# Scores' PSUM as one tile of two banks with a single buffer, in a two-layer hybrid attention backbone

## The chip, the cores and the metric

The kernel runs on one core of one Trainium2 chip. The metric is the device time of one execution in microseconds (us), as a median of several runs. PE is the matmul engine (TensorE; PEld is its weight loads, which overlap it), DVE the vector engine, ACT the scalar engine, POOL is GpSimd, and SP issues the DMAs. Scores are accumulated in PSUM, which here holds eight banks of 2 KB in each partition.

## The reference

Two layers (`DEPTH = 2`) work on 256 latent tokens and 256 context tokens of width 1024. Each projects its modulated input once and gives the columns to three groups of heads. Their outputs are concatenated, projected by `w_out` and followed by a convolutional FFN. The last layer computes latent tokens alone.

```python
def _diff_attend(q, k, v, lam, scale):                       # A: 6 heads, two maps per head, 32 wide
    s = jnp.einsum('bhqcd,bhkcd->bhcqk', q, k) * scale
    p = jax.nn.softmax(s, axis=-1)
    p = p[:, :, 0] - lam * p[:, :, 1]
    return jnp.einsum('bhqk,bhkd->bhqd', p, v)

# B: 6 heads, 64 wide, neighbourhood window with a bias, and all context keys, in one softmax
s = jnp.concatenate([s_win + bias (masked), s_ctx], axis=-1)
p = jax.nn.softmax(s, axis=-1)

# C: 4 heads, 96 wide, from low-rank q and kv
s = jnp.einsum('bhqd,bhkd->bhqk', q, k) * scale
p = jax.nn.softmax(s, axis=-1)
```

## The kernel before

**Stages.** Each layer first computes the modulation and the input projections, then attends in the order C, A, B, and then multiplies with `w_out` and runs the FFN. Every large product in split precision is three matmuls (`mm3`, lines 134 to 136): high by high, low by high, high by low. Group A has three pairs of heads `i`, whose two maps per head count as the two banks of a group. Group B has three pairs, whose two heads are the banks. Group C has two pairs.

**A scores group.** For one block of 128 queries `score3` issues six matmuls, three for each bank. The two banks' matmuls use different rows of the matmul array (32 or 64 of 128). Then comes, for each bank, a softmax (`softmax_rows`): DVE takes the negated maximum (L381), ACT the exponential with its row sum (L384), DVE the reciprocal (L385) and the scaling (L674; in A L701 to L703 instead, which put the two maps together). In B, latent queries first get the bias added in PSUM (L745). PE then transposes the probabilities (L392), ACT copies them out of PSUM (L393), and PE multiplies them with v (L400). A group is 512 keys wide for latent queries and 256 for context queries, which only layer 0 has.

**PSUM.** The eight banks are shared among four tags: `acc` three, `ada` one, `sc` two, `tp` two. Each call of `scp()` takes the next of the two `sc` banks, and waits until whoever used it last has read it:

```python
    def bank(tag, bufs):
        return ps.tile([P, 512], F32, tag=tag, name=tag, bufs=bufs)
...
    def scp():
        return bank("sc", 2)
```

The two banks also serve `proj_vk` (four token blocks), the early projections behind the FFN and the context modulation `evb`.

**Order.** A scheduler decides where each instruction stands on its engine. It knows the tiles and their buffers and fills the time between the dependent steps of attention with matmuls that wait for nothing: projections of the next pairs in A (the 256- or 512-column `acc` products), and the `w_out` products (`acc<-whi,mixhi` and their kin) in B. An engine runs its instructions strictly in that order.

Of the kernel before, what the change touches and what calls it, by code (L numbers as in the profile page):

```python
# [8 lines left out]
F32 = mybir.dt.float32  # L9
# [20 lines left out]
CTX, LAT = slice(0, 256), slice(256, 512)  # L30
# [47 lines left out]
def build(nc, tc, st, I, out):  # L78
    P = 128
# [9 lines left out]
    ps = st.enter_context(tc.tile_pool(name="ps", bufs=1, space=PSUM))  # L89
    dp = st.enter_context(tc.tile_pool(name="dp", bufs=1, space=bass.MemoryType.DRAM))  # L90

    V, S, G, T = nc.vector, nc.scalar, nc.gpsimd, nc.tensor

    def bank(tag, bufs):
        return ps.tile([P, 512], F32, tag=tag, name=tag, bufs=bufs)

    def acc():
        return bank("acc", 3)
# [2 lines left out]
        return bank("ada", 1)  # L101

    def scp():
        return bank("sc", 2)

    def tpp():
        return bank("tp", 2)

    def load(dst, src):
        nc.sync.dma_start(out=dst, in_=src)  # L110
# [14 lines left out]
    def split_from(src, hi, lo):  # L125
        S.copy(hi, src)
        V.tensor_tensor(lo, src, hi.bitcast(F32), ALU.subtract)
# [5 lines left out]
    def mm3(o, lh, ll, rh, rl, first, last):  # L133
        T.matmul(o, lhsT=lh, rhs=rh, start=first, stop=False)  # L134
        T.matmul(o, lhsT=lh, rhs=rl, start=False, stop=False)  # L135
        return T.matmul(o, lhsT=ll, rhs=rh, start=False, stop=last).ins  # L136
# [21 lines left out]
    LO, HI = list(range(4)), list(range(4, KD))  # L158
    early = {}
# [107 lines left out]
    def pump(n):  # L267
        while n and pend:
            try:
                next(pend[0])  # L270
                n -= 1
            except StopIteration:
                pend.pop(0)
# [105 lines left out]
    def softmax_rows(sc, nk, ap, tag):  # L379
        nm = sm.tile([P, 1], F32, tag="nm", name="nm")  # L380
        V.reduce_max(nm, sc[:, 0:nk], axis=AX.X, negate=True)  # L381
        p = ap.tile([P, 512], F32, tag=tag, name="p", bufs=2)
        sums = sm.tile([P, 2], F32, tag="sums", name="sums")
        hT["exp"] = S.activation(p[:, 0:nk], sc[:, 0:nk], AF.Exp, bias=nm, accum_out=sums[:, 0:1]).ins  # L384
        V.reciprocal(sums[:, 1:2], sums[:, 0:1])  # L385
        return p, sums
# [53 lines left out]
    def split_early(raw):  # L440
        hi = lp.tile([P, 1280], F32R, tag="ehi", name="ehi", bufs=2)
        lo = lp.tile([P, 1280], F32R, tag="elo", name="elo", bufs=2)
        split_from(raw, hi, lo)
        return kview((hi, lo), 2)
# [45 lines left out]
    nxt = load_round(1)  # L490
    ada_round(0, raws)
    ef = [acc() for _ in EF]
    evb = {pr: scp() for pr in (1, 0)}
    for s in range(4):
        ks = (2 * s, 2 * s + 1)
        w = split_early(wes[s])
# [39 lines left out]
    for l in range(L):  # L536
        last = l == L - 1
# [15 lines left out]
        pr = sm.tile([P, 2, 32], F32, tag="lampr", name="lampr", bufs=2)  # L553
# [43 lines left out]

        def proj_vk():
            w = vkw
            for t in (2, 3, 0, 1):  # L600
                tok = slice(128 * t, 128 * t + 128)
                po = acc() if last and t % 2 else scp()
                for k in range(KD):
                    hi, lo = w[k // 3 * 3]
                    mm3(po[:, 0:288], hT["hi"][:, k, tok], hT["lo"][:, k, tok], hi[:, k % 3, :], lo[:, k % 3, :],
                        k == 0, k == KD - 1)
                pump(PF)
                S.copy(vt[:, t, 256:544], po[:, 0:288])
# [13 lines left out]
        def score3(banks, q, k, rows, r0, qs, nk):  # L622
            for t, (a, b) in enumerate(((0, 0), (0, 1), (1, 0))):
                for n, sc in enumerate(banks):
                    r = slice(r0 + rows * n, r0 + rows * n + rows)
                    T.matmul(sc[:, 0:nk], lhsT=q[r, a, qs], rhs=k[r, b, 0:nk], start=t == 0, stop=t == 2,  # L626
                             tile_position=(r.start, 0))
# [39 lines left out]
        def simple_fin(k):  # L667
            def f(po, c):
                split_from(po, mix[0][:, k, c], mix[1][:, k, c])
            return f  # L670

        def normed(sc, nk):
            p, s = softmax_rows(sc, nk, ap, "p0")
            V.tensor_scalar_mul(p[:, 0:nk], p[:, 0:nk], s[:, 1:2])  # L674
            return p
# [19 lines left out]

        def attn_a(i):
            def sco(h, e, qs, qt, nk, name):
                banks = [scp() for _ in range(2)]
                score3(banks, aqs[i], aks[i], 32, 64 * e, qs, nk)
                (p0, s0), (p1, s1) = [softmax_rows(sc, nk, ap, f"p{m}") for m, sc in enumerate(banks)]  # L700
                V.tensor_tensor(s1[:, 1:2], s1[:, 1:2], lam[:, 2:3], ALU.mult)  # L701
                V.tensor_scalar_mul(p1[:, 0:nk], p1[:, 0:nk], s1[:, 1:2])
                V.scalar_tensor_tensor(p0[:, 0:nk], p0[:, 0:nk], s0[:, 1:2], p1[:, 0:nk], ALU.mult, ALU.add)  # L703
                return p0

            def fin(po, c):
                sq = ap.tile([P, 256], F32, tag="sq", name="sq", bufs=2)
                S.activation(sq, po, AF.Square)
                pm = tpp()
                T.matmul(pm[:, 0:256], lhsT=K["bones"], rhs=sq, start=True, stop=True)  # L710
                S.activation(sq, pm[:, 0:256], AF.Ln, bias=epsc)
                S.activation(sq, sq, AF.Exp, scale=-0.5)
                V.scalar_tensor_tensor(sq, po, nw[:, 0:1], sq, ALU.mult, ALU.mult)
                split_from(sq, mix[0][:, i, c], mix[1][:, i, c])

            heads(i, sco, vt, 0, fin)
# [13 lines left out]
        def attn_b(i):  # L730
            banks = []

            def sco(h, e, qs, qt, nk, name):
                if e == 0:
                    banks[:] = [scp() for _ in range(2)]
                    score3(banks, bqs[i], bks[i], 64, 0, qs, nk)
                sc = banks[e]
                if name == "lat":
                    bt = ap.tile([P, 256], F32, tag="rpb", name="rpb", bufs=3)
                    load(bt, I["rpb"][l, h, qt])  # L740
                    b3 = bt.rearrange("p (a c) -> p a c", c=64)
                    with tc.issue_after(hT["pow"]):
                        G.tensor_tensor(b3, b3, K["m01"].unsqueeze(1).to_broadcast([P, 4, 64]), ALU.mult)
                    G.tensor_tensor(b3, b3, K["mneg"].unsqueeze(1).to_broadcast([P, 4, 64]), ALU.add)
                    V.tensor_tensor(sc[:, LAT], sc[:, LAT], bt, ALU.add)  # L745
                return normed(sc, nk)

            heads(i, sco, vt, 416 if i else 384, simple_fin(3 + i))
# [23 lines left out]
        mq, mk = [], []  # L772
# [53 lines left out]
                S.copy(mq[h // 2][64:96, h % 2, :], q[32 * h:32 * h + 32, qc])  # L826

        def attn_c(i):
            def sco(h, e, qs, qt, nk, name):
                sc = scp()  # L830
                T.matmul(sc[:, 0:nk], lhsT=mq[i][0:96, e, qs], rhs=mk[i][0:96, e, 0:nk], start=True, stop=True)  # L831
                return normed(sc, nk)

            heads(i, sco, vm, 0, simple_fin(6 + i))

# [93 lines left out]
        def post(pl, b, t):  # L929
            r = rsum[t]  # L930
            y, rs = pst.pop(t)
            hT["dv"] = V.scalar_tensor_tensor(xr[t], y, rs[:, 0:1], b, ALU.mult, ALU.add, accum_out=r[:, 2:3]).ins
            pst[t] = centred(xr[t], (r[:, 2:3], r[:, 3:4]), pl, jt(pl))
# [210 lines left out]
        if not last:  # L1144
            free = [h1.tile([P, KD, 512], F32R, tag=n, name="ada" + n).bitcast(F32).rearrange("p k c -> p (k c)")
                    for n in ("hi", "lo")]
            sc = Slices(free[0], [free[1][:, 1024 * i:1024 * i + 1024] for i in range(4)])
# [9 lines left out]
        def tail2(ts):  # L1157
            if last:
                return
            for t in ts:  # L1160
                post(pq, b2, t)
            hold = ExitStack()
            if 2 in ts:
                flush()
                new_h()
            else:
                for i in (12, 13, 14):
                    w = kview(wsplit(I["w_f"][l + 1, i], 1024), KD)
                    early[i] = (acc() if i < 14 else scp(), w, [(CTX, LO + HI)] if i == 14 else [])
                    f_mm(early[i][0], w, 0, LO + HI, LAT, True, i < 14)  # L1170
                w = {kb: kview(wsplit(I["w_v"][l + 1, 0, kb], 1024), 4) for kb in range(2)}
                early["v"] = ({1: scp(), 0: acc()}, w, LO + HI, (0,))
                for e in range(2):
                    r = v_mm(early["v"][0][1], w, LO + HI, 1, e, True, True)
                hold.enter_context(tc.issue_after(r))
            with hold:
                for t in ts:
                    modulated(pq, l + 1, False, t, xr[t], sums=pst.pop(t))
# [101 lines left out]
```

## Time and profile before

| | |
|---|---|
| median of 3 runs | 1155.72 us (1154.95 to 1156.66) |
| profiled execution | 1158.58 us, of which 1156.5 us are the span of its trace |
| PE busy | 1107.0 us, 96% of the span |
| DVE, ACT busy | 836.1 us (72%), 591.2 us (51%) |
| mean granted PE clock | 0.986 of full speed |

PE is busy nearly all the time, so what counts is which of its time is useful, and where the other engines would hold it up. Busy time of PE includes the modelled end of each matmul; from start to start the same matmuls take a little less. In layer 0 attention lies between 118 and 316.5 us (C to 159.3, A to 261.7, B to 316.5), in layer 1 A and B lie between 824.9 and 943.2 us.

### The profile page before, as it was taken

What the parts mean: (1) busy time and instruction counts of PE and PEld (TensorE: products, weight loads), DVE (VectorE), ACT (ScalarE), POOL (GpSimd) and SP (SyncE); (2) the same over time, 40 slices, a digit from 0 to 9 for tenths busy, and PEclk for the clock granted to TensorE, in tenths of its full rate; (3) what the DMA queues carried; (4) which work ended last, traced back from release to release, by engine and by line L of the source; (5) the groups of instructions that cost most, each with busy time, mean ns of one, the idle gap of its engine ahead of it and who ended that gap; (6) DMA issues with size and microseconds to landing.
All of it is one profiled execution on the core that took longest, in us unless ns stands there. A gap on an engine that the chain in (4) does not pass through costs nothing.

```text
span 1156.5 us, 17907 instructions
## 1 busy us (share of the span) xinstructions
PE 1107.0 (96%) x6776; PEld 902.1 (78%) x6776; DVE 836.1 (72%) x1505; ACT 591.2 (51%) x1063; POOL 83.8 (7%) x104
## 2 busy tenths in 40 slices
PE   5999999999998999999999999999999979999997
PEld 3877666686778888887888877897778758999985
DVE  4544677757588887986977687666766777888755
ACT  4345556656548644444352245555555656666541
POOL 0000100003123000000000002110000420000000
PEclk9999999999999999999999999998999988999999
DMA  9767112112143554643558894533111333555662
GB/s 362 295 241 279 58 37 74 37 37 86 51 164 97 197 169 144 199 152 116 186 174 309 311 328 131 176 94 99 53 55 56 128 132 121 183 183 188 201 203 89
DMA packets 58213, 179.19 MB, mean 155 GB/s; under 512 B 7024, under 2 KB 12432, under 8 KB 58128
## 3 DMA queue, kind: packets, MB, share of 16 engines
q1 hardware_dynamic: 58128, 178.05, 45.8%
q8 instruction: 54, 0.88, 0.3%
q14 instruction: 31, 0.25, 0.1%
HBM read 176.94 MB, written 1.08 MB: 154 GB/s over the span
## 4 chain that ended last, share of the span: by engine, by line
PE 85%; DVE 6%; ACT 2%; issue 2%; POOL 2%; DMA 2%; SPq 0%; DVEq 0%; POOLq 0%; ACTq 0%
PE acc L134 21%; PE acc L135 21%; PE acc L136 21%; PE sc L626 6%; PE tp L392 3%; PE tp L400 3%; PE sc L831 2%; DVE wlo L122 1%; PE sc L134 1%; PE sc L135 1%; PE sc L136 1%; POOL xn L344 1%; DMA rawr<-in_w_ada_e 1%; PE ada L234 1%; PE ada L136 1%
## 5 line engine op out<-in xcount | busy, mean ns | idle before, releaser
L121 ACT CAST whi<-raw 128x1024 fp32r<-128x1024 f32 (+3 forms) x204 | 212.0, 1043 | 248.7 <-PE acc L135 124.4
L122 DVE TENSOR_TENSOR wlo<-raw,whi 128x1024 fp32r<-128x1024 f32 (+3 forms) x204 | 248.4, 1221 | 121.4 <-ACT whi L121 117.1
L134 PE MATMUL acc<-hhi,whi 128*128 128x256 f32 (+1 forms) x960 | 327.3, 341 | 3.5 <-ACT hhi L360 3.5
L135 PE MATMUL acc<-hlo,whi 128*128 128x256 f32 (+1 forms) x960 | 325.4, 339 | 0.5 <-DVE hlo L361 0.3
L136 PE MATMUL acc<-hhi,wlo 128*128 128x256 f32 (+1 forms) x960 | 324.1, 338 | 0.4 <-DVE wlo L122 0.4
L134 PEld LDWEIGHTS acc<-hhi,whi 128*128 128x128 f32 x960 | 184.7, 193 | 28.2 <-issue 5.4
L135 PEld LDWEIGHTS acc<-hlo,whi 128*128 128x128 f32 x960 | 184.9, 193 | 22.2 <-issue 3.6
L136 PEld LDWEIGHTS acc<-hhi,wlo 128*128 128x128 f32 x960 | 184.6, 192 | 22.1 <-issue 3.8
L384 ACT ACTIVATE p<-sc,nm 128x512 f32<-128x512 f32 (+1 forms) x132 | 81.4, 619 | 26.0 <-DVE nm L381 24.5
L381 DVE TENSOR_REDUCE nm<-sc 128x1 f32<-128x512 f32 (+1 forms) x132 | 77.3, 598 | 22.7 <-PE sc L626 15.9
L393 ACT COPY pT<-tp 128x512 f32<-128x512 f32 (+1 forms) x96 | 49.4, 516 | 56.2 <-PE tp L392 55.8
L626 PE MATMUL sc<-stk,stq 32*128 32x512 f32 (+3 forms) x324 | 75.0, 392 | 1.0 <-ACT p L384 0.9
L626 PEld LDWEIGHTS sc<-stk,stq 32*128 32x128 f32 (+1 forms) x324 | 41.6, 183 | 26.4 <-issue 11.5
L1064 ACT ACTIVATE u<-acc,conv 128x256 f32<-128x256 f32 (+1 forms) x94 | 60.8, 647 | 1.4 <-PE acc L136 1.3
L1067 DVE SCALAR_TENSOR_TENSOR u<-acc,conv,u 128x255 f32<-128x255 f32 (+1 forms) x94 | 55.1, 586 | 6.3 <-ACT u L1064 6.3
L1068 DVE SCALAR_TENSOR_TENSOR u<-acc,conv,u 128x255 f32<-128x255 f32 (+1 forms) x94 | 55.4, 589 | 2.3
L215 DVE SCALAR_TENSOR_TENSOR ac<-raw,scT,ac 128x1024 f32<-128x1024 f32 x42 | 53.4, 1281 | 4.7 <-DMA raw<-in_w_ada 4.6
L392 PE MATMUL tp<-ident,p 128*128 128x128 f32 x320 | 52.6, 279 | 0.6 <-DVE p L674 0.5
L392 PEld LDWEIGHTS tp<-ident,p 128*128 128x128 f32 x320 | 36.8, 140 | 20.8 <-issue 8.5
L134 PE MATMUL acc<-whi,gBhi 128*128 128x512 f32 x133 | 52.0, 392 | 0.0
L135 PE MATMUL acc<-wlo,gBhi 128*128 128x512 f32 x133 | 51.9, 390 | 0.0
L136 PE MATMUL acc<-whi,gBlo 128*128 128x512 f32 x133 | 51.8, 391 | 0.0
(282 smaller groups left out, 1816.6 us busy)
## 6 DMA issues: line engine op xcount, KB each, us to landing
raw<-in_w_up SPq DMA_DIRECT2D x94, 512.0 KB
raw<-in_w_down SPq DMA_DIRECT2D x53, 512.0 KB
adalo<-in_w_ada SPq DMA_DIRECT2D x32, 512.0 KB
raw<-in_w_f SPq DMA_DIRECT2D x27, 512.0 KB
rawr<-in_w_ada SPq DMA_DIRECT2D x24, 512.0 KB
raw<-in_w_ada SPq DMA_DIRECT2D x24, 512.0 KB
raw<-in_w_out SPq DMA_DIRECT2D x16, 512.0 KB
rawr<-in_w_ada_e SPq DMA_DIRECT2D x12, 512.0 KB
```

The lines of the kernel that those rows point to most:

```text
L121: S.copy(hi, raw)
L122: V.tensor_tensor(lo, raw, hi.bitcast(F32), ALU.subtract)
L134: T.matmul(o, lhsT=lh, rhs=rh, start=first, stop=False)
L135: T.matmul(o, lhsT=lh, rhs=rl, start=False, stop=False)
L136: return T.matmul(o, lhsT=ll, rhs=rh, start=False, stop=last).ins
L381: V.reduce_max(nm, sc[:, 0:nk], axis=AX.X, negate=True)
L384: hT["exp"] = S.activation(p[:, 0:nk], sc[:, 0:nk], AF.Exp, bias=nm, accum_out=sums[:, 0:1]).ins
L392: T.transpose(pt[:, 128 * kc:128 * kc + 128], p[:, 128 * kc:128 * kc + 128], ident)
L626: T.matmul(sc[:, 0:nk], lhsT=q[r, a, qs], rhs=k[r, b, 0:nk], start=t == 0, stop=t == 2, tile_position=(r.start, 0))
L1064: S.activation(t, po[:, c], AF.Identity, scale=cw[:, 1:2], bias=cw[:, 3:4])
L1067: V.scalar_tensor_tensor(t3[:, :, 1:], p3[:, :, 0:255], cw[:, 0:1], t3[:, :, 1:], ALU.mult, ALU.add)
L1068: V.scalar_tensor_tensor(t3[:, :, 0:255], p3[:, :, 1:], cw[:, 2:3], t3[:, :, 0:255], ALU.mult, ALU.add)
```

## The change

`scp()` hands out one tile of 4 KB, that is both banks, as a list of two halves, and there is one such buffer. Every caller takes both at once. `attn_c` issues the two heads' matmuls together, as A and B already did by their code. The bytes of PSUM are the same, and so is the number of instructions.

```diff
     def scp():
-        return bank("sc", 2)
+        t = ps.tile([P, 1024], F32, tag="sc", name="sc", bufs=1)
+        return [t[:, 0:512], t[:, 512:1024]]
...
-    evb = {pr: scp() for pr in (1, 0)}
+    evb = dict(zip((1, 0), scp()))
...
+            pos = []
             for t in (2, 3, 0, 1):
                 tok = slice(128 * t, 128 * t + 128)
-                po = acc() if last and t % 2 else scp()
+                if not pos:
+                    pos = scp()
+                po = acc() if last and t % 2 else pos.pop(0)
...
             def sco(h, e, qs, qt, nk, name):
-                banks = [scp() for _ in range(2)]
+                banks = scp()
                 score3(banks, aqs[i], aks[i], 32, 64 * e, qs, nk)
...
                 if e == 0:
-                    banks[:] = [scp() for _ in range(2)]
+                    banks[:] = scp()
                     score3(banks, bqs[i], bks[i], 64, 0, qs, nk)
...
             def sco(h, e, qs, qt, nk, name):
-                sc = scp()
-                T.matmul(sc[:, 0:nk], lhsT=mq[i][0:96, e, qs], rhs=mk[i][0:96, e, 0:nk], start=True, stop=True)
-                return normed(sc, nk)
+                if e == 0:
+                    banks[:] = scp()
+                    for n, sc in enumerate(banks):
+                        T.matmul(sc[:, 0:nk], lhsT=mq[i][0:96, n, qs], rhs=mk[i][0:96, n, 0:nk], start=True, stop=True)
+                return normed(banks[e], nk)
...
+                e14, ev = scp()
```

The order of instructions moves with it. On PE, in B of layer 0 (a pair of heads after the first, its two blocks of latent queries), stands before:

```order
L626 MATMUL sc<-stk,stq 128x512 x3
L392 MATMUL tp<-ident,p 128x128 x2
L626 MATMUL sc<-stk,stq 128x512 x3
L392 MATMUL tp<-ident,p 128x128 x2
L400 MATMUL tp<-pT,vt 64x128 x8
L134 MATMUL acc<-whi,mixhi 128x512
L135 MATMUL acc<-wlo,mixhi 128x512
L136 MATMUL acc<-whi,mixlo 128x512
L134 MATMUL ada<-whi,mixhi 128x512
L135 MATMUL ada<-wlo,mixhi 128x512
L136 MATMUL ada<-whi,mixlo 128x512
L626 MATMUL sc<-stk,stq 128x512 x3
```

and in the same place now (line numbers are up by four at the scores, by one in the helpers):

```order
L630 MATMUL sc<-stk,stq 128x512 x6
L393 MATMUL tp<-ident,p 128x128 x2
L401 MATMUL tp<-pT,vt 64x128 x8
L393 MATMUL tp<-ident,p 128x128 x4
L630 MATMUL sc<-stk,stq 128x512 x6
L393 MATMUL tp<-ident,p 128x128 x8
L630 MATMUL sc<-stk,stq 128x256 x6
L393 MATMUL tp<-ident,p 128x128 x4
```

The two halves of a group stand together, and the `w_out` products between the groups are gone from this stretch. Over the program the scores of A and B stand in 88 pieces before (60 in layer 0, 28 in layer 1) and in 54 pieces of six now (36 and 18). Of the `w_out` products of layer 0, 72 start within or just behind B before; now 54 stand within A and 30 within B.

On DVE, in the same place (the bias, the maxima, and what follows for the first latent group of a pair), stands before:

```order
L745 TENSOR_TENSOR sc<-sc,rpb 128x256 x2
L381 TENSOR_REDUCE nm<-sc 128x1 x2
L127 TENSOR_TENSOR mixlo<-tp,mixhi 128x256
L385 RECIPROCAL sums<-sums 128x1
L674 TENSOR_SCALAR p<-p,sums 128x512
L385 RECIPROCAL sums<-sums 128x1
L674 TENSOR_SCALAR p<-p,sums 128x512
```

and now:

```order
L749 TENSOR_TENSOR sc<-sc,rpb 128x256
L382 TENSOR_REDUCE nm<-sc 128x1
L128 TENSOR_TENSOR mixlo<-tp,mixhi 128x256
L386 RECIPROCAL sums<-sums 128x1
L749 TENSOR_TENSOR sc<-sc,rpb 128x256
L678 TENSOR_SCALAR p<-p,sums 128x512
L382 TENSOR_REDUCE nm<-sc 128x1
L386 RECIPROCAL sums<-sums 128x1
L678 TENSOR_SCALAR p<-p,sums 128x512
```

The bias and the maximum of the second head moved behind the reciprocal of the first head, which needs that head's exponential. In A and C the maximum of the second bank stands behind the first bank's reciprocal in the same way. On ACT, in these latent groups of B, a copy of transposed probabilities (L394) now stands between the two exponentials of a group, where both exponentials stood together before.

## Rows read from the trace of the kernel before

**Rows 1.** The page, parts 1 and 2: busy time by engine, and granted clock.
```profile
PE 1107.0 (96%) x6776; PEld 902.1 (78%) x6776; DVE 836.1 (72%) x1505; ACT 591.2 (51%) x1063; POOL 83.8 (7%) x104
PEclk9999999999999999999999999998999988999999
```
**Rows 2.** The page, part 4: chain that ended last, by engine.
```profile
PE 85%; DVE 6%; ACT 2%; issue 2%; POOL 2%; DMA 2%; SPq 0%; DVEq 0%; POOLq 0%; ACTq 0%
```
**Rows 3.** Windows: stretch and length, busy us of each engine, clock, DMA share, GB/s.
```profile
118.00:159.30 41.30, 40.97 (x236) 28.30 (x232) 26.78 (x70) 21.73 (x57) 3.25 (x4) 1.00 0.17 52
159.30:261.70 102.40, 102.40 (x611) 73.53 (x610) 75.28 (x204) 61.58 (x159) 0.00 (x0) 1.00 0.14 47
261.70:316.50 54.80, 53.56 (x382) 38.02 (x380) 38.18 (x94) 32.41 (x86) 14.48 (x18) 1.00 0.23 71
...
824.90:895.40 70.50, 70.18 (x461) 54.67 (x460) 48.46 (x109) 39.07 (x86) 0.00 (x0) 1.00 0.16 55
895.40:943.20 47.80, 47.74 (x315) 34.98 (x314) 36.62 (x71) 28.14 (x55) 14.80 (x18) 1.00 0.44 146
```
**Rows 4.** The same windows, scores' line L626 alone: PE and PEld busy.
```profile
159.30:261.70 102.40, 32.55 (x144) 19.07 (x144) 1.00 0.14 47
261.70:316.50 54.80, 14.15 (x72) 8.05 (x72) 1.00 0.23 71
...
824.90:895.40 70.50, 18.99 (x72) 9.85 (x72) 1.00 0.16 55
895.40:943.20 47.80, 9.35 (x36) 4.62 (x36) 1.00 0.44 146
```
**Rows 5.** Timeline of PE, three places in layer 0: start, length, what.
```profile
159.31 0.96 PE L626 MATMUL sc<-stk,stq 32*128 32x512 f32 x6
160.20 0.44 PE L392 MATMUL tp<-ident,p 128*128 128x128 f32 x2
...
170.03 0.96 PE L626 MATMUL sc<-stk,stq 32*128 32x512 f32 x3
170.92 0.66 PE L392 MATMUL tp<-ident,p 128*128 128x128 f32 x4
...
308.57 0.62 PE L626 MATMUL sc<-stk,stq 64*128 64x256 f32 x6
```
**Rows 6.** Chain of waits in layer 1: start, time on the chain, what.
```profile
872.76 0.79 ACT p L384 x2
...
873.60 1.63 PE sc L626 x6
...
877.38 0.31 PE acc L134
877.69 0.12 PE acc L135
```
**Rows 7.** Timeline in layer 1: a piece of scores on PE, its maximum on DVE.
```profile
831.89 0.96 PE L626 MATMUL sc<-stk,stq 32*128 32x512 f32 x3
...
832.89 0.69 DVE L381 TENSOR_REDUCE nm<-sc 128x1 f32<-128x512 f32 x1 [0.40 <-PE sc L626]
```
**Rows 8.** Timeline of ACT and DVE, a latent group of B in layer 0.
```profile
281.59 0.70 ACT L384 ACTIVATE p<-sc,nm 128x512 f32<-128x512 f32 x1
...
284.28 0.59 ACT L393 COPY pT<-tp 128x512 f32<-128x512 f32 x1 [0.30 <-PE tp L392]
...
282.41 0.17 DVE L385 RECIPROCAL sums<-sums 128x1 f32<-128x1 f32 x1 [0.26 <-ACT p L384]
282.61 0.49 DVE L674 TENSOR_SCALAR p<-p,sums 128x512 f32<-128x512 f32 x1
```
**Rows 9.** The bias line L745: shortest, median and longest of its instructions, in ns.
```profile
L745 DVE TENSOR_TENSOR sc<-sc,rpb x24: 417/432/433, 262.8 to 929.9; 128x256 f32<-128x256 f32 x24
```
**Rows 10.** Windows behind attention of layer 0 and round a stop, as rows 3.
```profile
349.40:353.00 3.60, 1.77 (x12) 1.57 (x13) 3.60 (x8) 3.57 (x9) 0.00 (x0) 1.00 0.05 16
353.00:356.50 3.50, 3.50 (x19) 3.50 (x18) 3.18 (x7) 0.54 (x2) 1.52 (x1) 0.51 0.00 0
```

More of the change, by code (lines that the diff above doesn't have):

```diff
@@ L828, in attn_c @@
         def attn_c(i):
+            banks = []
             def sco(h, e, qs, qt, nk, name):
-                sc = scp()
-                T.matmul(sc[:, 0:nk], lhsT=mq[i][0:96, e, qs], rhs=mk[i][0:96, e, 0:nk], start=True, stop=True)
-                return normed(sc, nk)
+                if e == 0:
[3 more added lines that the diff above has]
+                return normed(banks[e], nk)
             heads(i, sco, vm, 0, simple_fin(6 + i))
@@ L1166, in tail2 @@
             else:
+                e14, ev = scp()
                 for i in (12, 13, 14):
                     w = kview(wsplit(I["w_f"][l + 1, i], 1024), KD)
-                    early[i] = (acc() if i < 14 else scp(), w, [(CTX, LO + HI)] if i == 14 else [])
+                    early[i] = (acc() if i < 14 else e14, w, [(CTX, LO + HI)] if i == 14 else [])
                     f_mm(early[i][0], w, 0, LO + HI, LAT, True, i < 14)
                 w = {kb: kview(wsplit(I["w_v"][l + 1, 0, kb], 1024), 4) for kb in range(2)}
-                early["v"] = ({1: scp(), 0: acc()}, w, LO + HI, (0,))
+                early["v"] = ({1: ev, 0: acc()}, w, LO + HI, (0,))
                 for e in range(2):
```

## The prediction

> **What bounds the kernel now.** The busy shares come first: PE works 96% of the span, DVE 72%, ACT 51% [rows 1], and the chain that ended last runs over PE for 85% of the time [rows 2]. So a saving must be PE time, and a loss must be PE standing still. Next come the windows by stage. In A of both layers PE is busy almost without a gap (102.40 of 102.40 us, 70.18 of 70.50), in B of layer 0 nearly so (53.56 of 54.80), at the full clock [rows 3]. A group's softmax passes DVE, ACT and DVE again, which costs nothing today because PE has other matmuls to do meanwhile: projections in A, `w_out` products in B. Third come the same windows for the scores' line alone: 32.55 + 14.15 + 18.99 + 9.35 = 75.0 us of PE [rows 4].
>
> Those 75.0 us hold a waste, which the timeline shows. Where the six matmuls of a group stand together, the two banks' halves run side by side in the array: 159.31 to 160.20, 0.89 us for a 512-wide group. Where three stand alone they take the same 0.89 us (170.03 to 170.92), for half a group [rows 5].
>
> **Pairing: -27 us.** The new order has each of the 54 groups of A and B in one piece. Of these 36 are 512 wide (12 in A and 6 in B of each layer), 18 are 256 wide (12 and 6, layer 0). At 0.89 and about 0.55 us (0.62 with its modelled end of 0.07, which 0.96 against 0.89 shows too [rows 5]) they need 36 x 0.89 + 18 x 0.55 = 42. Before, 75.0 less 88 pieces x 0.07 = 69. The gain is 27, of which 12.4 in A and 4.2 in B of layer 0, and 10.4 in layer 1. It is sure only while both banks are free when the six are issued, which a single buffer guarantees. Bounds: 22 to 28, since some pieces before ran halves together by luck of the queue.
>
> **Fewer changes of mode: -4 us.** The first 256-column matmul behind scores takes 0.31 us, the next 0.12 [rows 6]. There are 34 pieces fewer. Were each followed by such a product it would be 34 x 0.19 = 6.5; transposes stand behind many, so I take 4 (0 to 6.5).
>
> **What the single buffer adds.** Now the next group's scores wait for both exponentials of the last one, and with six in one row everything behind them in PE's queue waits too. I follow one 512-wide group of A from the start of its scores: first maximum after 1.00 [rows 7], which takes 0.69; exponential to reciprocal 0.82, reciprocal to the next DVE step 0.20 [rows 8]; only then the second maximum, 0.69; second exponential to the next scores 0.84 [rows 6]. That makes 4.24 us, and about 3.0 (estimate) for a 256-wide group. PE's own part of it is 0.89, so 3.3 us must be filled by transposes, products with v and projections.
>
> *A and C of layer 0, +10 us.* Twelve groups of 4.24 and twelve of 3.0 make 87 us in a window of 102, of which the other matmuls of A fill 102.4 - 32.6 = 70 [rows 3, 4], together with the 54 `w_out` products that were moved there. In the first two pairs of heads I find enough of them behind each group. The end of the last pair has between none and four products of 0.24 us (twice the 0.12 of 256 columns [rows 6]) behind a context group, and each of some eight groups leaves about 1 us open; 2 more are lost singly in A and C. Bounds: 3 (the queue runs ahead) and 18 (gaps in the other pairs too).
>
> *B of layer 0, +20 us.* This is the term that decides. In a latent group the chain has the bias as well, twice 0.43 [rows 9], and the first head's scaling, 0.49, before the second maximum: 1.00 + 0.43 + 0.69 + 0.82 + 0.20 + 0.43 + 0.49 + 0.69 + 0.84 = 5.6 us. ACT now copies the first head's transposes (0.59 [rows 8], behind 0.5 of PE) before the second exponential, which moves that by 0.4: 6.0. In the first latent group of a pair the first exponential stands behind the `mixhi` cast, which waits for the last pair's products with v: 6.7. The context groups come to 3.7 and 3.3 by the same links at 256 columns, the first behind eight transposes. A pair of heads is then 19.7 us, three are 59, with the entry 60, against 54.8 now. And of 72 `w_out` products in this window only 30 are left. PE's work in it would be 54.8 - 4.2 - 42 x 0.24 = 40, so it stands still for 20. The lower bound is 10, if the second bias and maximum start early enough that a latent group takes 4.4; the upper is 28, if transposes and v products wait one more time in each group.
>
> *A and B of layer 1, +5 us.* There are no context queries, eighteen groups of 4.2 to 6.0 us stand in 118.3 us [rows 3], and products lie between nearly all of them; the walk leaves 5 open (2 to 10).
>
> *Small ones.* In `proj_vk` of layer 0 the third block now waits for the copies of the first two, 0.5 (0 to 1); in layer 1 the `acc` banks cover it. `evb`, the early projections and C issue the same matmuls; the bias tiles come late nowhere, since a latent group is now longer. The 12 `w_out` products that ran earlier are counted where they stand.
>
> *The clock, +3 us.* Between 349.4 and 353.0 PE was busy for 1.77 of 3.60 us, and the next 3.5 us had a granted clock of 0.51, the lower of its two levels, 1.2 GHz [rows 10]. In B of layer 0, PE would stand still in much the same share of each latent group. A fall of 3.5 us costs about half of what PE does in it, 1 to 2 us. I take two falls (0 to 12, the latter if most of the six latent groups run at half).
>
> **Sum.** -27 - 4 + 10 + 20 + 5 + 0.5 + 3 = +7.5 us. The profiled execution took 1158.6, of which 2.1 lie outside the span, and stands 2.9 above the median; what holds for it holds for the median: 1155.7 + 7.5 = 1163.
>
> **A rule against the change.** The row says that the end of one group and the start of the next overlap today, since the second exponential of a group (872.76, with its sum read) is followed at once by scores for the bank that it freed, while the other bank is still at work [rows 6]. The Trainium skill, Perfetto Trace Analysis, section "Matmuls", advises that independent groups of matmuls rotate through different PSUM banks, so that emptying one overlaps the next group's matmuls; with this change groups no longer do so. By the rule alone the loss would be the open part of every chain, 36 x 3.3 + 18 x 2.4 = 162 us (worked out from the links above); by the rows most of that is covered by other matmuls, and the sum holds 35 of it.
>
> **Rivals.**
> 1. *Pairing wins: faster.* In B the scheduler's order is the same, but the links are shorter than my walk: if PE's queue runs on so that a pair of heads takes 16 us instead of 19.7, B gives back 11, and with 5 instead of 10 open in A the time is 1155.7 + 7.5 - 11 - 5 = 1147. It decides from 17.2 us for a pair, where the sum is zero. For it speaks that a pair takes 18.3 now with twice the matmuls in it; against it, that the second maximum stands behind the first reciprocal on DVE.
> 2. *The clock falls through most of B.* 12 instead of 3 gives 1172. For it speaks that the latent groups have no `w_out` products between them any more; against it, that PE would still have 40 us of work in the 60 of B. Beside it, the Trainium skill, TensorE: Matmul & The Clock Gate, section "A second HAM failure mode: psum-queue depth-cycling", tells of a kernel whose clock went up and down because PE idled briefly between groups of matmuls on cycling PSUM buffers; no row here shows that in attention, where PE has no gaps yet.
> 3. *The waits show in all of A and in layer 1.* With 18 and 10 instead of 10 and 5 the time is 1176. The rows of A speak against it, 70 us of other matmuls beside the scores.
> 4. *Gain and loss cancel.* If each term is off by a little, or the scheduler's walk already balanced them, the time is within 0.2% of the old one, 1153.4 to 1158.0, which is about what a measurement can tell from no change.
>
> **Chances.** The forecast (1158 to 1169) 0.42, rival 1 0.27, rival 2 0.10, rival 3 0.07, rival 4 0.14. So faster by over 0.2%: 0.27; within: 0.14; slower: 0.59. From 1147 to 1174 leaves out rival 3 and the far side of rival 1, about 2 in 10.
>
> **What would show it.** Right: L626's successor busy for 45 to 47 us (with modelled ends) instead of 75 in the four windows; B of layer 0 near 60 us with PE idle a third of it, the scores' weight loads waiting for the exponential; A and B of layer 1 together some 8 us shorter than 118.3; a lower clock somewhere in B of layer 0. Wrong: PE as dense in B as before, or a second maximum that starts before the first exponential ends; or groups of six that take longer than 0.89, since then the pairing gain was never there.

## The result and the profile after

The changed kernel takes 1193.17 us (median of 4 runs, 1190.99 to 1197.06) against 1155.66 us: a ratio of 1.033 (95% interval 1.030 to 1.036), 37.5 us slower. The direction of the forecast was right, the size far off: 1163 was predicted, with 1174 as the upper end. The profiled execution took 1190.99 us, 32.4 more than that of the kernel before; the traces can account for these 32.4, and not for the 5 that the medians differ by beyond them.

First the page of the changed kernel, busy time, granted clock in 40 slices, and the chain that ended last by engine, beside [rows 1, 2]:

```profile
PE 1096.0 (92%) x6776; PEld 894.8 (75%) x6776; DVE 835.0 (70%) x1505; ACT 590.4 (50%) x1063; POOL 84.8 (7%) x104
PEclk9999999996789999999999999999999987999998
PE 74%; DVE 12%; ACT 7%; issue 3%; POOL 2%; DMA 2%; SPq 0%; DVEq 0%; ACTq 0%; POOLq 0%
```

PE is busy for 11 us less, so there is a saving. But the chain has left PE for DVE and ACT in 12 + 7% of the span where it was 6 + 2%, and the clock now falls in slices 10 to 12 of 29.7 us (A's end and B of layer 0), where it held before. The fall in slices 33 and 34 (from the end of layer 1's attention on) was there before too, at 0.8 and 0.8 instead of 0.8 and 0.7 [rows 1].

The windows by stage, as [rows 3]: C and A of layer 0, B of layer 0, A of layer 1, and B of layer 1 up to 973.40, where seven `w_out` products that follow without a gap are still to come.

```profile
118.40:159.87 41.47, 41.24 (x249) 30.44 (x246) 27.95 (x76) 23.04 (x58) 1.73 (x2) 1.00 0.20 64
159.87:273.67 113.80, 103.79 (x653) 75.30 (x652) 76.44 (x198) 61.84 (x160) 0.00 (x0) 0.96 0.16 52
273.67:344.50 70.83, 49.32 (x317) 34.00 (x317) 34.45 (x93) 28.92 (x80) 13.53 (x18) 0.73 0.10 32
853.73:921.40 67.67, 65.17 (x462) 50.51 (x462) 47.18 (x104) 37.86 (x84) 0.00 (x0) 1.00 0.18 56
921.40:973.40 52.00, 45.87 (x309) 33.85 (x308) 34.74 (x68) 29.16 (x57) 15.48 (x18) 0.93 0.37 119
```

And the scores' line alone (L630 now) in the last four of them, as [rows 4]:

```profile
159.87:273.67 113.80, 19.36 (x144) 11.04 (x144) 0.96 0.16 52
273.67:344.50 70.83, 12.88 (x72) 7.39 (x72) 0.73 0.10 32
853.73:921.40 67.67, 11.55 (x72) 5.79 (x72) 1.00 0.18 56
921.40:973.40 52.00, 6.11 (x36) 2.96 (x36) 0.93 0.37 119
```

The scores' PE time fell from 75.0 to 49.9 us, as the pairing term said. In B of layer 0, PE stands still for 70.83 - 49.32 = 21.5 us, as the stall term said. What neither says is the clock of 0.73 there, for which the prediction had two short falls.

A second latent group of B, on all engines (timeline of the changed kernel, start and length), shows the chain link by link:

```profile
306.21 1.65 PE L630 MATMUL sc<-stk,stq 64*128 64x512 f32 x6 [1.41 <-ACT p L385]
307.79 1.11 PE L393 MATMUL tp<-ident,p 128*128 128x128 f32 x4
307.96 0.43 DVE L749 TENSOR_TENSOR sc<-sc,rpb 128x256 f32<-128x256 f32 x1 [1.08 <-PE sc L630]
308.42 0.69 DVE L382 TENSOR_REDUCE nm<-sc 128x1 f32<-128x512 f32 x1
308.99 0.58 ACT L394 COPY pT<-tp 128x512 f32<-128x512 f32 x1 [2.84 <-PE tp L393]
309.47 0.69 ACT L385 ACTIVATE p<-sc,nm 128x512 f32<-128x512 f32 x1
310.29 0.17 DVE L386 RECIPROCAL sums<-sums 128x1 f32<-128x1 f32 x1 [1.17 <-ACT p L385]
310.37 0.43 DVE L749 TENSOR_TENSOR sc<-sc,rpb 128x256 f32<-128x256 f32 x1
310.71 0.83 DVE L678 TENSOR_SCALAR p<-p,sums 128x512 f32<-128x512 f32 x1
311.46 0.68 DVE L382 TENSOR_REDUCE nm<-sc 128x1 f32<-128x512 f32 x1
311.69 1.09 PE L393 MATMUL tp<-ident,p 128*128 128x128 f32 x4 [2.79 <-DVE p L678]
312.87 0.58 ACT L394 COPY pT<-tp 128x512 f32<-128x512 f32 x1 [2.61 <-PE tp L393]
313.35 0.69 ACT L385 ACTIVATE p<-sc,nm 128x512 f32<-128x512 f32 x1
314.19 0.58 PE L630 MATMUL sc<-stk,stq 64*128 64x256 f32 x2 [1.41 <-ACT p L385]
```

The group takes 314.19 - 306.21 = 7.98 us; the walk of the prediction said 6.0. Its order of steps is right. Three links are longer. The first bias starts 1.75 after the scores instead of 1.00, because the six matmuls take 1.58 (to 307.79) instead of 0.89. The first exponential stands behind a copy of transposes of the group before, 0.36 more. The second exponential starts 1.89 after the second maximum instead of 0.69 + 0.4, since the transposes take 1.1 instead of 0.5. The clock explains the first and most of the third: 0.89 and 0.5 are times at the upper level, and 1.58 and 1.1 come from a stretch at 0.50. Two windows of that stage of the changed kernel and the PE timeline of its last pair of heads show it:

```profile
311.20:314.60 3.40, 1.50 (x8) 1.13 (x10) 1.27 (x4) 1.26 (x3) 2.29 (x4) 0.50 0.13 39
...
324.80:328.20 3.40, 2.83 (x23) 2.00 (x20) 2.43 (x6) 1.22 (x4) 1.39 (x2) 1.00 0.59 186
```
```profile
323.18 0.96 PE L630 MATMUL sc<-stk,stq 64*128 64x512 f32 x6
...
329.95 0.99 PE L630 MATMUL sc<-stk,stq 64*128 64x512 f32 x6 [1.41 <-ACT p L385]
```

Where the clock is at its upper level, 2.4 GHz, a first latent group takes 329.95 - 323.18 = 6.77, the 6.7 of the walk. At 1.2 GHz (0.50) PE's steps in the chain take longer. B of layer 0 has four stretches at that level, and the end of one that began in A; here are the four (windows):

```profile
278.50:292.10 13.60, 9.82 (x32) 6.03 (x32) 6.49 (x14) 5.09 (x12) 5.73 (x8) 0.50 0.09 29
299.00:302.40 3.40, 2.99 (x22) 1.86 (x18) 1.12 (x2) 0.73 (x3) 0.19 (x1) 0.50 0.13 39
305.80:319.40 13.60, 8.99 (x54) 6.92 (x56) 5.97 (x16) 4.50 (x13) 4.54 (x6) 0.50 0.06 19
333.10:339.90 6.80, 4.40 (x26) 3.48 (x28) 2.60 (x8) 2.32 (x6) 0.00 (x0) 0.50 0.00 0
```

### The profile page after: what moved, and what is told of

Same layout as the page of the kernel before. It is cut to its first block, busy times and chain, and to the rows that moved or that the text cites. A ratio compares the mean times of both kernels' runs of the same rounds, so it can differ in the third digit from the quotient of the medians.

```text
span 1189.0 us, 17878 instructions
## 1 busy us (share of the span) xinstructions
PE 1096.0 (92%) x6776; PEld 894.8 (75%) x6776; DVE 835.0 (70%) x1505; ACT 590.4 (50%) x1063; POOL 84.8 (7%) x104
## 4 chain that ended last, share of the span: by engine, by line
PE 74%; DVE 12%; ACT 7%; issue 3%; POOL 2%; DMA 2%; SPq 0%; DVEq 0%; ACTq 0%; POOLq 0%
PE acc L135 18%; PE acc L137 18%; PE acc L136 18%; PE tp L393 4%; PE tp L401 4%; DVE wlo L123 3%; PE sc L630 2%; ACT p L385 2%; ACT whi L122 2%; PE sc L839 1%; DVE p L707 1%; PE sc L135 1%; PE sc L136 1%; PE ada L235 1%; PE sc L137 1%
## 5 line engine op out<-in xcount | busy, mean ns | idle before, releaser
L135 PE MATMUL acc<-hhi,whi 128*128 128x256 f32 (+1 forms) x960 | 323.4, 337 | 3.5 <-ACT hhi L361 3.5
L394 ACT COPY pT<-tp 128x512 f32<-128x512 f32 (+1 forms) x96 | 49.2, 513 | 97.6 <-PE tp L393 97.4
L386 DVE RECIPROCAL sums<-sums 128x1 f32<-128x1 f32 x132 | 21.4, 162 | 86.9 <-ACT p L385 86.7
L393 PE MATMUL tp<-ident,p 128*128 128x128 f32 x320 | 58.6, 302 | 23.7 <-DVE p L678 17.1
L630 PE MATMUL sc<-stk,stq 32*128 32x512 f32 (+3 forms) x324 | 49.9, 415 | 13.5 <-ACT p L385 13.4
```

Of the source, the lines that this page charges most:

```text
L393: T.transpose(pt[:, 128 * kc:128 * kc + 128], p[:, 128 * kc:128 * kc + 128], ident)
```

## The experiments

All were compared with the kernel before on the same chip in the same hour; its medians were 1155.3 for the first four experiments, 1156.7 for the next four and 1155.1 for the last three. Four theories were on trial: the order within a group's chain (1), that is the second bank's maximum behind the first bank's reciprocal, called the tie below; the release of both banks at once (2); the clock (3); and the tile of 4 KB as such (4).

**Both maxima first.** In the source, both biases and both maxima stand ahead of the first exponential; one tile, one buffer.

```diff
-                (p0, s0), (p1, s1) = [softmax_rows(sc, nk, ap, f"p{m}") for m, sc in enumerate(banks)]
+                nms = [neg_max(sc, nk) for sc in banks]
+                (p0, s0), (p1, s1) = [softmax_rows(sc, nk, ap, f"p{m}", nms[m]) for m, sc in enumerate(banks)]
...
```


> The changed kernel, with both banks' bias additions and both maxima issued ahead of the first exponential. Theory 1 (the order within the chain: the second bank's bias and maximum behind the first bank's reciprocal make the long group): a latent group of B falls from 7.9 us to about 6.5, a pair of heads from 24.8 to about 21, and A's end and layer 1 gain a few us too: 1193 becomes 1175 to 1182. Theory 2 (the release: the next scores wait for both exponentials, whatever stands between): within 4 us of 1193.

1170.47 us, ratio 1.014 (1.012 to 1.016): 23 us of the 37.5 came back, more than theory 1 asked for, and theory 2 alone is out. Layer 1, from its first A scores to the transposes ahead of the FFN, took 122.0 us (127.1 before the change, 131.8 after it).

**Two tiles instead of one.**

```diff
-        t = ps.tile([P, 1024], F32, tag="sc", name="sc", bufs=1)
-        return [t[:, 0:512], t[:, 512:1024]]
+        return [ps.tile([P, 512], F32, tag=f"sc{n}", name="sc", bufs=1) for n in range(2)]
```


> The changed kernel, but the two halves are two tiles of 2 KB with tags and single buffers of their own; the callers still take both at once, and C still issues both heads together. Theories 1 and 2 (both need the one tile): back to 1153 to 1159, with scores of A and B in pieces of three again. Rival (the callers: C's pairing, the third block of the early projection, the early blocks behind the FFN): stays above 1165.

1157.72 us, ratio 1.002 (1.001 to 1.003). C's pairing and the callers that take two banks at once cost about 2 us together (0.8 to 3.6 by the interval); the rest of the 37.5 sits in the one tile. The maxima stood together on DVE again, though the source is the same.

**PE kept busy in B of layer 0.**

```diff
+        if warm is not None:
+            for _ in range(6 if nk == 512 else 2):
+                T.matmul(pt, lhsT=warm[:, 0, 0:128], rhs=warm[:, 0, :], start=True, stop=True)
...
```


> The changed kernel, with matmuls whose result is overwritten ahead of each transpose of B in layer 0 (6 of 512 columns for a latent block, 2 for a context block; 96 in all, 22 us of PE at full clock), to keep PE busy while it waits. Theory 3 (the low clock in B lengthens the chain itself: scores 1.58 instead of 0.89, transposes 1.1 instead of 0.6): granted clock in B back near 1, B from 71 us to 60 to 63, total 1183 to 1187. If the low clock only goes along with the waits: no gain, 1191 to 1200.

1184.80 us, 8.4 less than the changed kernel, although 96 matmuls were added. The stretch of B's scores in layer 0, first the changed kernel and then this one (windows):

```profile
273.70:341.50 67.80, 46.29 (x300) 31.75 (x300) 32.76 (x88) 27.09 (x74) 13.53 (x18) 0.71 0.11 33
```
```profile
273.10:330.20 57.10, 55.15 (x377) 38.06 (x379) 32.19 (x88) 26.75 (x74) 14.09 (x18) 0.99 0.11 31
```

At a clock of 0.99 the same chain takes 57.1 us instead of 67.8. Nine of the 18 `w_out` products moved out of the stretch too, worth up to 4 us of it (estimate: twice the 0.23 from one start to the next at the upper clock, for each product), so the clock's part is 7 to 11.

**`w_out` products held behind B's first scores.**

```diff
...
+                    if not last and jb in (3, 0):
+                        hold.enter_context(tc.issue_after(firstb[2 if jb == 3 else 0]))
...
```


> The changed kernel, with the early w_out products of layer 0 held behind the first scores of B, so that none of the 54 stands in A and they lie in B. If B is long because its fillers were used up in A: A's last pair gets longer by up to 4 us beside the 13 that it loses in work, B gets its cover and its clock back, total 1183 to 1188. If the fillers only move the same idle time from one place to the other: within 4 us of 1193.

1186.60 us, 6.6 less. B's scores took 61.1 us with a clock of 0.90; but A took 116.9 without any of the 54 products, where it took 113.8 with them, and its clock was 0.85. Which stage has the filling work matters somewhat. The larger part of the loss is there with either.

**Both maxima first and PE kept busy**, the two edits together.

> Both maxima first, as in the run before last of that name, and the overwritten matmuls in B of layer 0 too. If the low clock still costs in B of layer 0 when the chain is shorter (scores 1.58 us there instead of 0.89): 1170.5 becomes 1162 to 1166, with a pair of heads at 18 to 19 us. If a short chain no longer suffers from it: 1169 to 1174.

1172.92 us: no gain over 1170.47, although the clock in B rose from 0.80 to 0.97. B took 62.3 us instead of 63.7. In the kernel with the maxima first PE stands still for 16.2 us of it, less than the 22 us that the added matmuls need at the full clock by the estimate above, so they may cost what the clock gives back; this is argued. What the low clock costs a group without the tie was thus not measured.

**Pairs by order, in two tiles.** The second bank, which comes free last, goes first, and all other matmuls of the group stand behind its first one.

```diff
-                for n, sc in enumerate(banks):
+                    for n in (1, 0):
...
+                        if t == 0 and n == 1 and (True):
+                            both.enter_context(tc.issue_after(m.ins))
```


> Two tiles of 2 KB with tags of their own, and the six matmuls of each group of A and B kept together by order alone: the second bank's first matmul goes ahead of all others, so a group still waits for both exponentials, but the two halves are no longer one tile. Theory 2 (the wait for both exponentials is the rest of the loss once the maxima stand first): 1163 to 1172, like the kernel with both maxima first. Theory 4 (the one tile costs by itself, through what the scheduler ties to it, beyond the order of the maxima): 1150 to 1160.

1146.46 us, ratio 0.991 (0.989 to 0.992): faster than the kernel before by 0.9%. Of the 54 groups of A and B 47 go as one set of six here too, behind both exponentials; in the other seven the first matmul or the first few go up to 2 us ahead of the rest. So theory 2 falls: the wait for both banks is more than paid by the pairing. Theory 4 stood, and the timelines say how. Here are DVE and ACT in a latent group of B, first of the kernel with both maxima first (one tile), then of this one:

```profile
314.39 1.29 DVE L382 TENSOR_REDUCE nm<-sc 128x1 f32<-128x512 f32 x2
...
315.71 0.69 ACT L389 ACTIVATE p<-sc,nm 128x512 f32<-128x512 f32 x1 [0.47 <-DVE nm L382]
```
```profile
275.16 1.29 DVE L381 TENSOR_REDUCE nm<-sc 128x1 f32<-128x512 f32 x2
...
276.11 0.69 ACT L384 ACTIVATE p<-sc,nm 128x512 f32<-128x512 f32 x1
```

With one tile the first exponential starts when both maxima are done (314.39 + 1.29 = 315.68), though it needs one. With two tiles it starts before that (276.11 against 276.45). This holds throughout: with one tile and the maxima first, the first exponential starts at least 0.03 us behind the end of the second maximum in all 66 groups of A, B and C; with two tiles it starts ahead of that end in 47 of 66. So ACT's use of one half waits for DVE's use of the other half, in the order of the source. In the changed kernel the source has the first exponential ahead of the second maximum, and DVE must wait for ACT: there the second maximum starts at least 0.20 us behind the end of the first exponential in all 66 groups. That the program's dependences are kept by tile, even between two reads, is argued from this and from the order, which goes back when the tile is split; the list of dependences itself was not seen.

**Pairs except in B of layer 0, and in layer 1 alone.** The last kernel with a condition on the order's edge:

```diff
-                        if t == 0 and n == 1 and (True):
+                        if t == 0 and n == 1 and (last or rows == 32):
...
+                        if t == 0 and n == 1 and (last):
```


> As the last, but B of layer 0, where there is little else to do on PE, lets each bank go by itself. If pairing pays where other matmuls cover the wait (A of both layers, B of layer 1) and loses in B of layer 0 alone: 1146 to 1153. If the other matmuls that A then uses up are missing in B all the same: 1155 to 1162.

> As the last, with pairs kept together in layer 1 alone. Layer 1 of the kernel with both maxima first took 122.0 us from its first A scores to the transposes ahead of the FFN, before it was 127.1: so 1150 to 1153. If that gain came from the shorter DVE order and not from pairing: 1154 to 1158.

1142.95 us, ratio 0.988 (0.987 to 0.990), the fastest of all; and 1151.38 us, ratio 0.996 (0.994 to 0.998). Pairing is worth 5 us in layer 1 and 8 in A of layer 0, and costs 3.5 in B of layer 0, where PE has least else to do.

**The tie by order, with and without pairs.** In two tiles, the second bank's bias and maximum are put behind the first bank's reciprocal by order.

```diff
-        V.reciprocal(sums[:, 1:2], sums[:, 0:1])
+        hT["rcp"] = V.reciprocal(sums[:, 1:2], sums[:, 0:1]).ins
...
+                with tc.issue_after(hT["rcp"]):
+                    p1, s1 = softmax_rows(banks[1], nk, ap, "p1")
...
```


> Two tiles of 2 KB, pairs kept together by order (that kernel took 1146.5 us), and by order too the second bank's bias and maximum behind the first bank's reciprocal, as one tile has them. Theory 1 (this order in the chain is what the one tile costs; the joint release costs nothing beyond it): 1185 to 1197, like the changed kernel. Theory 2 (the release of both halves at once, or something else in a tile of 4 KB): 1146 to 1160.

> Two tiles of 2 KB, each bank released by itself and scores free to go in pieces of three, with only the order of the second bank's steps behind the first bank's reciprocal. Theory 1: the longer chain of a group costs here too, but a bank that is free early lets the next scores start: 1162 to 1180. If the tie matters only where both banks must be free: 1153 to 1160.

With pairs 1194.39 us (ratio 1.034, 1.033 to 1.036), which is the changed kernel to 0.1%; without pairs 1165.56 us (1.009, 1.008 to 1.011). So the four corners are: neither 1157.7, pairs alone 1146.5, the tie alone 1165.6, both 1194.4. The tie costs 8 us where a bank that is free early lets three matmuls go, and 48 where all six wait for its end. Two tiles with the same order are as slow as the one tile, so the tile of 4 KB costs through the order that it brings, and theory 4 needs nothing beyond it.

**One bias and one maximum for both banks**, in one tile.

```diff
+        nm = sm.tile([P, 2], F32, tag="nm", name="nm")
+        V.reduce_max(nm, both[:, :, 0:nk], axis=AX.X, negate=True)
...
```


> One tile of 4 KB with one buffer, as in the changed kernel, but one bias addition and one maximum over both banks in a single instruction each, so that nothing on DVE stands between the exponentials. The first exponential then waits for the maximum of both, 0.6 us later than it has to. Theory 1 with this remainder: between the kernels with both maxima first (1170.5) and with pairs by order (1146.5), 1155 to 1170. If one tile is slow whatever stands in the chain: above 1170.

1162.59 us (1.006, 1.005 to 1.008), in the middle of what theory 1 gave. One tile is not slow whatever stands in the chain, but the first exponential still waits for both maxima. That this wait makes all of the 16 us to the kernel with pairs by order was not tried.

## Why the prediction failed

- **Pairing, -27.** Right: 75.0 - 49.9 = 25.1 us of the scores' PE time [rows 4], and groups of six at 0.89 us at the upper clock. The prediction's sign was 45 to 47 us; the 3 above it stand in B of layer 0 (12.88, where the six 512-wide groups at 0.96 and six 256-wide at 0.62 make 9.5), at the low clock.
- **Fewer changes of mode, -4.** Its reading does not hold. The 0.31 us of the first 256-column product, where the next takes 0.12, was put down to the scores in front of it. In the trace of the kernel before, a first 512-column product of attention starts 0.34 us ahead of the next behind scores, 0.34 behind products with v and 0.32 behind transposes, where 0.23 is usual in a row of products. So most of the excess is no matter of the scores, and no run shows the 4.
- **Stalls in A and C, +10.** Right: 113.80 - 103.79 = 10.0 in A and 0.2 in C, against 0.0 and 0.3 before [rows 3].
- **Stalls in B of layer 0, +20.** Right: 21.5. The walk's 6.7 for a first latent group was 6.77 at the upper clock, and with the clock held B took 57.1 up to the scores of its last group, where the walk makes 59 - 3.3 = 56.
- **The clock, +3. This is the term that failed.** It was sized by two falls of 3.5 us. At a mean of 0.73, B of layer 0 ran (1 - 0.73) x 2 x 70.8 = 38 us at 1.2 GHz. PE's work there is 49.3 us where the prediction had 40, while PE stands still about as long as forecast: so nearly all of the 10.8 us by which B is longer than 60 is PE's work at the lower clock. The point against rival 2, PE's 40 us of work in the 60 of B, did not hold. Nor was it counted that PE's scores and transposes are links of the waiting chain, which is longer at the lower level: 7.98 instead of 6.0. Over the whole trace, stretches at 0.50 make 84.4 us with PE busy for 55.5 of them, against 32.1 and 19.6 before; at half of PE's work, the prediction's own price, that is 18 us more (estimate) where 3 was put. Holding the clock in B alone gave back 8.4 us net. A's end (0.96) and the end of layer 1 (0.93) had falls too, which no experiment priced. Rival 2 had this mechanism at a chance of 0.10 and at 1172, for B alone.
- **A and B of layer 1, +5 beside -10.4. The net is wrong in sign.** PE stood still for 67.67 - 65.17 + 52.00 - 45.87 = 8.6 us, some 3 more than sized, and the clock fell in B, where it had held before. From the first A scores to the transposes ahead of the FFN it is 131.8 instead of 127.1 where some 120 was forecast. With the maxima first it is 122.0, so nearly all of the excess comes with the tie.
- **Front, +0.5.** Right: A starts at 159.87 instead of 159.31 [rows 5].
- **The reason that was given.** The prediction put the loss on the single buffer, that is on the wait for both exponentials. The runs say otherwise: with that wait and without the tie the kernel is 10 us faster than before. The second maximum behind the first reciprocal was in the walk as a row of the order and was taken as given. It was the cause, 48 us where all six matmuls wait and 8 where they do not, and rival 1 ("the second maximum stands behind the first reciprocal" as the point against it) named it without pricing it by itself.
- **The rule on rotating banks.** The Trainium skill (Perfetto Trace Analysis, section "Matmuls") was set against the change with 162 us for all open chains. Its direction held for the change (37.5 us slower), but pairs by order rotate no more than the changed kernel does, or hardly more, and win (1146.46 us). What this case measures is that the wait for both banks pays over the whole kernel once the tie is gone, though it costs 3.5 us in B of layer 0.
- **What stays open.** The trace is 32.5 us longer, with PE 11.0 less busy and 43.5 longer idle; the terms made 28 less busy and 35.5 longer idle. So 17 of the 25 that are missing are PE's work and 8 its idle time. In layer 0 the terms made +13.7 with the clock's 3, and it was 212.8 - 184.3 = 28.5. The clock in B explains 7 to 11 of it, the falls in A's end a few. In layer 1, of some 11 us between forecast and measurement 3 are idle time in A and B, 2 idle time behind the last `w_out` product (10.36 us to the transposes instead of 8.60), and 6 PE's work, of which the clock explains about half; the rest was not separated. Nor was it tried to hold the clock in all stages at once.

## What to carry to other kernels

A tile can also be the unit in which dependences are kept, as the order of all 66 groups suggests here: before joining two buffers into one, ask which engines touch the halves in turn, and price each step that the join puts behind another engine's, since it may cost far more than the shared release. If buffers shall be used together, an order of instructions does it without joining them. And when PE starts to wait on a chain that has PE's own short steps in it, price those steps at the lower clock too: the falls came with the waits here, 84 us at the lower level against 32 before.

## What was not expected of the hardware

Two windows of the whole stage show what holding two banks together can give when nothing is tied: layer 0 from the first A scores to the transposes ahead of the FFN, and layer 1 likewise, for the kernel with pairs by order.

```profile
159.14:336.37 177.23, 171.13 (x1105) 124.29 (x1104) 137.69 (x344) 103.08 (x261) 17.82 (x23) 0.99 0.23 76
819.20:941.16 121.96, 108.54 (x775) 82.78 (x774) 93.54 (x196) 70.55 (x147) 20.17 (x23) 0.98 0.30 93
```

They were 184.3 and 127.1 us in the kernel before. PE has more idle time here than there and is still done earlier. The clock was the other surprise: it fell to 0.50 again and again, for 38 of 70.8 us in B, though PE was busy for 26.2 of the 37.4 us in the four stretches shown above.
